# Hybrid encoder layer: the per-head norm of the delta-rule branch summed through VectorE's 32x32 block turn, its later steps ordered behind the solver's instructions, and one tile moved to another ring

## Chip, cores and metric

The kernel runs on one core of one Trainium2 chip. The metric is the device time of one execution in microseconds (us); the median of several runs counts. A core has five engines that run side by side, each through its own instructions in a fixed order: TensorE (PE in the profile, with its weight loads listed apart as PEld), VectorE (DVE), ScalarE (ACT), GpSimd (POOL) and SyncE (SP), which here issues nearly all DMAs.

## The reference

One encoder layer for 512 tokens (two sequences of 256) of 1024 channels, in f32. After an RMS norm and one wide projection come three branches: A, a bidirectional gated delta rule with 8 heads of 128 channels; B, multi-head latent attention with 8 heads and a rotary part; C, cross-attention into 256 memory tokens with 4 heads. Each branch is multiplied by a silu gate, projected, weighted by a sigmoid gate and summed; an output projection, the residual and a final norm follow. What the change is about is the norm at the end of branch A, over the 128 channels of each head and token:

```python
def _rmsnorm(x, gain):
    xf = x.astype(jnp.float32)
    y = xf * lax.rsqrt(jnp.mean(xf * xf, axis=-1, keepdims=True) + EPS)
    return (y * gain.astype(jnp.float32)).astype(x.dtype)
...
    o_gdn = _rmsnorm(o_fwd + o_bwd, gdn_norm_gain).reshape(b, s, W_GDN).astype(x.dtype) * jax.nn.silu(z_gdn)
```

## The kernel before

**Tiling.** Activations lie with channels on the 128 partitions and the 512 tokens along the row. Every projection (`gemm`, L262 to L279) is a set of 128x128 by 128x512 products. Each operand is split into a rounded high part and a low rest, and three products (high x high, low x high, high x low) are summed. For a weight tile ScalarE makes the high part (L241) and VectorE the low part (L244), just ahead of its products. These two steps are remembered as `self.wround` and `self.wsplit`.

**Stages.** `front` does the memory branch, the norms, the decay terms and the latent attention. `middle` does the delta rule with projections woven in. `back` does the last projections and the output. Queues of ready projections (`fills`, `weave`) are put between the dependent steps so that TensorE always has work.

**Order.** In `front` and `back` a scheduler orders each engine's instructions by priority and by a timeline that it estimates. In `middle` TensorE's order is written by a planner, `weave`: each chain of steps is a generator, whose `yield a, b` says that its products cost `a` us of TensorE and that the chain may go on `b` us after them; in between, products from the queue are placed. The other engines are ordered by the scheduler, and the chains have priorities: solver lanes and `heads_out` 2000, `heads_norm` 1500, `heads_in` 300, `preps` 100, queue work below that. `tc.issue_after(x)` makes every instruction traced inside it stand behind `x` on the engine of `x`; it does not concern other engines.

**The chain of one head in `middle`.** `gdn_in` loads decay rows and values and makes the products `kk` (L1015), one group for each half sequence; VectorE multiplies them by decay factors into `ne` (L1025, four instructions a half), which frees the PSUM banks for the next `kk`. `gdn_solve` runs in two lanes (even and odd heads), with VectorE steps at L1117 and `w` at L1136 and ScalarE copies `ub` at L1144. `gdn_out` makes the head's output `o` (L1165), scales it by gain and gate into `og` (L1172), squares it (`sq`, L1174) and adds a small term (L1177). Then come the sums over channels: four products (L1181), one for each 128 tokens, with the squares as 128x128 weights and a column of ones as the moving operand. Their result is 128x4, tokens on partitions. VectorE scales it into `rr` (L1183), GpSimd raises it to the power -1/2 (L1184), VectorE turns `rr` by 32x32 blocks into `rt` (L318), and four DMAs (L320) write the 512 factors to DRAM. `gdn_norm` loads them back as a row on all partitions (`rob`, L324), multiplies (`og`, L1197, behind `wsplit`) and splits the product into `xg` (L252, L256), the operand of the branch's projection `gm_bg` (L1295, L1302, and L276 in `back`).

**Rings.** Scratch tiles of one tag share a ring of buffers: `tb` has 2, `s2` has 5. A new tile waits until all readers of the tile that had its buffer are done. `sq` and `rob` are `tb` tiles. So is `rps` in `decay_b` (L632), which holds the decay rows until DMAs (L638, L639) have written them to DRAM, and so are `rt` and `ru` in `mla_rope`, the rotary part of the queries of four heads. (The name `rt` is used for two tiles: this one, and the turned `rr`.)

**Rotary step.** `mla_rope(g)` makes two projections `ra`, `rb` and then two halves, each two rotations (L524), a sum (L694), a split (L252, L254) and six DMAs (L700 to L706). It is a generator: the second half is traced later, between the key and the query projection of the group's first head.

Of the kernel before, what the change touches and what calls it, by code (L numbers as in the profile page):

```python
# [181 lines left out]
class Layer:  # L182
# [131 lines left out]

    def store_cols(self, r, i):

        nc = self.nc
        nc.vector.transpose(out=self.rt, in_=r)  # L318
        for b in range(4):
            nc.sync.dma_start(self.d_n[i].rearrange("(j b i) -> b j i", j=4, b=4)[b], self.rt[32 * b:32 * b + 4])  # L320

    def load_row(self, dst, i):
# [268 lines left out]
    def decay_b(self):  # L591
# [21 lines left out]
        for s in range(2):  # L613
            for d in range(2):
# [12 lines left out]
                for tb in range(2):  # L627
                    for i in range(2):
                        nc.tensor.matmul(rp[:, s * 256:(s + 1) * 256], ga[:, i, tb],
                                         um[1 + d][:, 128:384] if tb == 0 else um[1 + d][:, 0:256],  # L630
                                         start=d + tb + i == 0, stop=d + tb + i == 3)
        rs = self.tb("rps")  # L632
        nc.scalar.activation(rs, rp, AF.Copy)
# [47 lines left out]
    def mla_rope(self, g):  # L681
# [6 lines left out]
        for j, (p1, p2, op) in enumerate(((pa, pb, ALU.subtract), (pb, pa, ALU.add))):  # L688
            if j:
                yield  # L690
            t, u = self.tb("rt"), self.tb("ru")
            self.rotate(t, unpaired(p1), self.cos)
            self.rotate(u, unpaired(p2), self.sin)
            nc.vector.tensor_tensor(t, t, u, op=op)  # L694
            hi = self.pa.tile([P, 512], F32R, tag="Qn", bufs=4, name=f"rh{g}{j}")
            lo = self.pa.tile([P, 512], F32R, tag="Qn", bufs=4, name=f"rl{g}{j}")
            with self.tc.issue_after(self.wround) if j else nullcontext():
                self.split(t, hi, lo)
            q1, q2, dq = qs1.bitcast(F32), qs2.bitcast(F32), self.d_q[g, j]
            nc.sync.dma_start(dq[0], hi.bitcast(F32))  # L700
            nc.sync.dma_start(dq[1], lo.bitcast(F32))
            for o in (32 * j, 64 + 32 * j):
                nc.sync.dma_start(q1[o:o + 32], dq[0].rearrange("(h r) t -> r h t", h=4))
            for a in range(2):
                o = 64 * a + 32 * j
                nc.sync.dma_start(q2[o:o + 32], dq[1, 64 * a:64 * a + 64].rearrange("(h r) t -> r h t", h=2))  # L706
        self.qs = qs1, qs2
        yield

# [274 lines left out]
    def gdn_in(self, hh):  # L984
# [23 lines left out]
        for s in range(2):  # L1008
# [9 lines left out]
            for d in range(2):  # L1018
                for cp in range(2):
                    cch = cp if d == 0 else 1 - cp  # L1020
                    w = 4 * h + 2 * s + cch
                    r = slice(256, 384) if cp else slice(0, 256)
                    kin = pc[cch][:, :, 128 * (1 - d):128 * (2 - d)] if cp else pc[cch]
                    n = 128 if cp else 256
                    nc.vector.scalar_tensor_tensor(  # L1025
                        ne[:, :, d, s, r], es[d][:, s, r].unsqueeze(1).to_broadcast([P, 2, n]),
                        cc[:, d, w:w + 1], kin, ALU.mult, ALU.mult)
        nc.gpsimd.tensor_tensor(v3, v3, nk[:, 4 * h:4 * h + 4].unsqueeze(2).to_broadcast([P, 4, P]), op=ALU.mult)  # L1028
# [3 lines left out]
    def gdn_solve(self, hh):  # L1032
# [72 lines left out]
        for cp in range(2):  # L1105
# [29 lines left out]
            wv = w2(f"w2{hh}{cp}")  # L1135
            nc.vector.tensor_tensor(wv, v4[:, :, 1 - cp], x3, op=ALU.subtract)  # L1136
            yield 0.45, 6.5
# [4 lines left out]
            for d in range(2):  # L1142
                t = slice(64 * (1 - d), 64 * (1 - d) + 64)
                nc.scalar.activation(ub[t, d, :, cp], u3[t], AF.Copy)  # L1144
            yield 0.45, 6.5
        self.ub[hh] = ub

    def gdn_out(self, hh):
# [28 lines left out]
        nc.vector.tensor_tensor(s3, s3, kq[:, :, 1], op=ALU.add)  # L1177
        yield 0.0, 13 if hh == 7 else 11
        ssp = self.ps_ms(par, f"so{hh}")
        for tb in range(4):  # L1180
            nc.tensor.matmul(ssp[:, tb:tb + 1], sq[:, tb * P:(tb + 1) * P], c("one"), start=True, stop=True)  # L1181
        rr = self.rr[:, 0:4]
        nc.vector.tensor_scalar(rr, ssp[:, 0:4], 1.0 / 128, 128 * EPS * EPS, ALU.mult, ALU.add)  # L1183
        nc.gpsimd.tensor_tensor(rr, rr, c("hf")[:, 0:4], op=ALU.pow)  # L1184
        self.store_cols(self.rr, hh)
        self.og[hh] = og, self.now + 10.0
        yield 0.9, 0.0

    def gdn_norm(self, hh):
# [5 lines left out]
        yield 0.0, 6.0 if hh == 7 else 12.0  # L1195
        with self.tc.issue_after(self.wsplit):
            nc.vector.tensor_tensor(og, og, rb, op=ALU.mult)  # L1197
        hl = self.pk.tile([P, 2, 512], F32R, tag="kq", bufs=8, name=f"xg{hh}")
        self.split(og, hl[:, 0], hl[:, 1], 0.5)
        self.xg[hh] = hl[:, 0], hl[:, 1]  # L1200
# [268 lines left out]
    def front(self):  # L1469
# [24 lines left out]
        self.mem_attn(3, *q)  # L1494
        rope = self.mla_rope(0)
        next(rope)
        for g in range(2):
            fills(1)
            self.mla_v(g)

            def between():
                next(rope)
                fills(1)

            nxt = self.mla_qk(4 * g, between)
            for h in range(4):
# [12 lines left out]
                if h == 3 and g == 0:  # L1519
                    rope = self.mla_rope(1)  # L1520
                    next(rope)
                    fills(1)
# [5 lines left out]
    def middle(self):  # L1528
# [6 lines left out]
        for j in range(2):  # L1535
# [4 lines left out]
            self.ym.append((y, m))  # L1540
        self.started, self.b0 = set(), None
        self.og, self.b0 = {}, self.blocks(0)
# [166 lines left out]
```

## Time and profile before

| what | value |
|---|---|
| median of 3 runs | 808.98 us (808.81, 808.98, 810.21) |
| profiled execution: its time | 810.45 us |
| profiled execution: span of its instructions | 808.6 us |
| granted TensorE clock over the span | 0.996 |
| busy share of the span: PE, PEld, DVE, ACT, POOL | 98%, 87%, 70%, 55%, 18% |
| DMA: moved, mean rate | 118.20 MB, 146 GB/s |

How to read the rows below. In a timeline, each row is: start in us, duration in us, engine, line of the kernel, operation, output<-inputs, shape, count (xN: N in a row, first start to last end); a bracket holds the idle time of the engine just before the row and what ended it. In a table of groups the figures after the bar are total busy us and mean ns of one instruction, then idle time before them. Waits are: engine and line, what it waited for, us in total, times, longest. Windows are: stretch, its length, then busy us and count for PE, PEld, DVE, ACT and POOL, then the granted TensorE clock, DMA share and GB/s. A product of f32 operands shows as two records, one of the rounded kind as one.

### The profile page before, as it was taken

The page shows a single profiled execution, that of the slowest core. Times are in us where ns is not written, and L with a number is a line of the kernel's source. Part 1 is how long each engine was busy: PE and PEld are TensorE (multiplying, and loading weights), DVE is VectorE, ACT ScalarE, POOL GpSimd, SP SyncE. Part 2 cuts the span into 40 slices and gives each one's busy share as a digit, 9 for nine tenths or more (in the row PEclk, how much of TensorE's full clock was granted, in tenths as well). Part 3 has the DMA queues.
Part 4 walks back from the last instruction along what each step waited for, and adds up shares of the span by engine and source line. Part 5 has one row for each costly group of instructions (what it writes and reads, how often), then busy time and mean ns, then how long its engine had stood idle before and what let it go on. Part 6 is the DMA issues. An engine that isn't in the chain of part 4 may idle for free.

```text
span 808.6 us, 13182 instructions
## 1 busy us (share of the span) xinstructions
PE 794.3 (98%) x4822; PEld 699.7 (87%) x4822; DVE 565.6 (70%) x957; ACT 448.8 (55%) x895; POOL 147.1 (18%) x135
## 2 busy tenths in 40 slices
PE   9999999999999999999999999999999999999996
PEld 7888888889898889988888878788888888888885
DVE  7786458688699999577699998666644654455543
ACT  7755455456565566648676748476755552222332
POOL 0200111000010002074032136214110002223221
PEclk9999999999999999999999999999999999999999
DMA  9422222552417625345344353736444557454532
GB/s 333 162 81 95 92 91 76 185 150 74 120 60 228 162 98 168 123 153 168 118 131 139 109 174 127 216 124 180 149 129 130 182 196 251 131 185 173 172 104 105
DMA packets 68913, 118.20 MB, mean 146 GB/s; under 512 B 23664, under 2 KB 31216, under 8 KB 68848
## 3 DMA queue, kind: packets, MB, share of 16 engines
q1 hardware_dynamic: 67552, 115.00, 45.2%
q10 hardware_dynamic: 1296, 2.36, 0.8%
q8 instruction: 38, 0.62, 0.3%
q14 instruction: 27, 0.22, 0.1%
HBM read 98.24 MB, written 19.09 MB: 145 GB/s over the span
## 4 chain that ended last, share of the span: by engine, by line
PE 86%; DVE 8%; DMA 2%; ACT 2%; issue 1%; SPq 0%; POOL 0%; POOLq 0%; DVEq 0%; ACTq 0%
PE gm_g L276 14%; PE gm_qkv L276 12%; PE gm_z L276 5%; PE gm_za L276 5%; PE gm_bm L276 5%; PE y L1328 4%; PE vm L429 3%; PE gm_be L276 3%; PE gm_qm L276 3%; PE gm_km L276 3%; PE gm_bg L276 3%; PE o L1165 2%; PE gm_bg L1295 2%; PE s_a L337 2%; PE kk L1015 2%; PE gm_qn L276 2%
## 5 line engine op out<-in xcount | busy, mean ns | idle before, releaser
L782 DVE SCALAR_TENSOR_TENSOR kq<-cz,prm,kq 128x510 f32<-128x510 f32 (+1 forms) x64 | 52.7, 823 | 3.7 <-ACT kq L775 2.9
L276 PE MATMUL gm_qkv<-hh,wh_qkv 128*128 128x512 f32 x192 | 49.2, 389 | 1.3 <-ACT wh_qkv L241 1.3
L276 PE MATMUL gm_g<-hh,wl_g 128*128 128x512 f32 x192 | 48.9, 384 | 0.0
L276 PE MATMUL gm_g<-hl,wh_g 128*128 128x512 f32 x192 | 48.1, 384 | 0.0
L276 PE MATMUL gm_g<-hh,wh_g 128*128 128x512 f32 x192 | 48.1, 385 | 0.0
L276 PE MATMUL gm_qkv<-hl,wh_qkv 128*128 128x512 f32 x192 | 47.7, 383 | 0.0
L276 PE MATMUL gm_qkv<-hh,wl_qkv 128*128 128x512 f32 x192 | 47.4, 383 | 0.0
L244 DVE TENSOR_TENSOR wl_g<-wr_g,wh_g 128x1024 fp32r<-128x1024 f32 x24 | 29.8, 1243 | 19.4 <-PE gm_g L276 10.2
L276 PEld LDWEIGHTS gm_qkv<-hh,wh_qkv 128*128 128x128 f32 x192 | 35.9, 192 | 6.5 <-ACT wh_qkv L241 1.7
L1025 DVE SCALAR_TENSOR_TENSOR ne<-e,cc,kk 128x512 f32<-128x512 f32 (+1 forms) x64 | 35.5, 607 | 8.3 <-PE kk L1015 5.6
L276 PEld LDWEIGHTS gm_qkv<-hh,wl_qkv 128*128 128x128 f32 x192 | 35.9, 189 | 4.9
L276 PEld LDWEIGHTS gm_qkv<-hl,wh_qkv 128*128 128x128 f32 x192 | 35.7, 189 | 4.7
L276 PEld LDWEIGHTS gm_g<-hl,wh_g 128*128 128x128 f32 x192 | 35.5, 189 | 4.8
L276 PEld LDWEIGHTS gm_g<-hh,wl_g 128*128 128x128 f32 x192 | 35.3, 189 | 4.5
L276 PEld LDWEIGHTS gm_g<-hh,wh_g 128*128 128x128 f32 x192 | 35.1, 189 | 4.6
L244 DVE TENSOR_TENSOR wl_qkv<-wr_qkv,wh_qkv 128x1024 fp32r<-128x1024 f32 x24 | 30.9, 1286 | 10.6 <-ACT wh_qkv L241 5.3
L1328 PE MATMUL y<-wh_wo,mh 128*128 128x512 f32 (+1 forms) x144 | 37.7, 356 | 0.0
L1270 POOL TENSOR_TENSOR mg<-mg,lg 128x512 f32<-128x512 f32 x16 | 27.0, 1695 | 50.5 <-DVE lg L1269 29.7
L241 ACT ACTIVATE wh_qkv<-wr_qkv 128x1024 fp32r<-128x1024 f32 x24 | 25.3, 1055 | 19.2 <-DMA wr_qkv<-in_w_dram 6.8
L241 ACT ACTIVATE wh_g<-wr_g 128x1024 fp32r<-128x1024 f32 x24 | 25.3, 1054 | 17.4 <-PE gm_g L276 12.4
L1028 POOL TENSOR_TENSOR vs<-vs,ns 128x512 f32<-128x512 f32 x8 | 8.5, 1065 | 128.0 <-DVE tt L911 84.4
L997 POOL TENSOR_TENSOR kl<-kq,kh 128x512 fp32r<-128x512 f32 x16 | 22.5, 1410 | 50.0 <-ACT kh L995 47.7
(453 smaller groups left out, 2187.5 us busy)
## 6 DMA issues: line engine op xcount, KB each, us to landing
wr_g<-in_w_dram SPq DMA_DIRECT2D x24, 512.0 KB
wr_qkv<-in_w_dram SPq DMA_DIRECT2D x24, 512.0 KB
e<-d_r SPq DMA_DIRECT2D x64, 96.0 KB
wr_z<-in_w_dram SPq DMA_DIRECT2D x12, 512.0 KB
d_g<-gt_g SPq DMA_DIRECT2D x16, 256.0 KB
wr_za<-in_w_dram SPq DMA_DIRECT2D x8, 512.0 KB
lg<-d_g SPq DMA_DIRECT2D x16, 256.0 KB
wr_bm<-in_w_dram SPq DMA_DIRECT2D x8, 512.0 KB
```

The costliest lines, as they stand in the source:

```text
L241: self.wround = nc.scalar.activation(hi[:, :n], raw[:, :n], AF.Copy).ins
L244: self.wsplit = nc.vector.tensor_tensor(lo[:, :n], raw[:, :n], hi[:, :n].bitcast(F32), op=ALU.subtract).ins
L276: nc.tensor.matmul(pairs(ps[:m]), a[:, k * m:(k + 1) * m], turns(xs[k][j]), start=n == 0, stop=n == 3 * nk - 1)
L337: nc.tensor.matmul(pairs(sp[:, qb * 256:(qb + 1) * 256]), a, turns(b), start=j == 0, stop=j == n - 1)
L429: nc.tensor.matmul(pairs(vps[tb]), ms[k][a][:, t], turns(b[:, :512]), start=k == 0 and i == 0, stop=k == 7 and i == 2)
L782: nc.vector.scalar_tensor_tensor(ys, zs, self.cw[:, f, m:m + 1], ys, ALU.mult, ALU.add)
L997: nc.gpsimd.tensor_tensor(lo, src, hi.bitcast(F32), op=ALU.subtract)
L1015: nc.tensor.matmul(pairs(ps), a[:, k], turns(b), start=i == 0, stop=i == 2)
L1025: nc.vector.scalar_tensor_tensor(ne[:, :, d, s, r], es[d][:, s, r].unsqueeze(1).to_broadcast([P, 2, n]), cc[:, d, w:w + 1], kin, ALU.mult, ...
L1165: nc.tensor.matmul(out, ub[:, d, s, cp], rhs, start=n == 0, stop=n == 3)
L1270: nc.gpsimd.tensor_tensor(self.merged[d], self.merged[d], gt, op=ALU.add)
L1328: nc.tensor.matmul(pairs(ps), xs[2 * j + q][a][:, t], turns(b[:, q * 512:(q + 1) * 512])[:, c0 // 2:c1 // 2], start=j == 0 and n == 0, sto ...
```

## The change

In `gdn_out` VectorE now turns the 128x512 squares by 32x32 blocks (`st`) and adds up each group of 32 along the row, which leaves 128x16 partial sums. One product with a 128x32 block-identity as weights adds the four partition groups, 32x16. The power step works on 32x16; the store becomes one turn of 32x32 and one DMA. The store is a step of its own, 4 us (head 7: 2 us) after the power step. The planner's waits change from 11 to 12 us before the product, and from 10 to 8 us before the row may be loaded; the product's stated cost falls from 0.9 to 0.25.

A list `kept` holds the last eight traced instructions of three kinds: `ne` (L1025), `w` (L1136) and the `ub` copies (L1144). `behind()` orders what is traced in it after `wsplit` and after all of these. It covers the turn and the sum, the turn of the factors, and in `gdn_norm` both the multiplication and the split.

`rps` moves from ring `tb` to ring `s2`. `mla_rope` is no longer a generator: both halves are traced at once, and the second one's split is no longer ordered behind `wround`.

```diff
-        rs = self.tb("rps")
+        rs = self.s2("rps")
...
         for j, (p1, p2, op) in enumerate(((pa, pb, ALU.subtract), (pb, pa, ALU.add))):
-            if j:
-                yield
...
-            with self.tc.issue_after(self.wround) if j else nullcontext():
-                self.split(t, hi, lo)
+            self.split(t, hi, lo)
...
-        yield 0.0, 13 if hh == 7 else 11
+        st = self.tb(f"st{hh}")
+        red = self.rr[:, 16:32]
+        with self.behind():
+            nc.vector.transpose(out=st, in_=sq)
+            nc.vector.tensor_reduce(red, st.rearrange("p (j i) -> p j i", i=32), axis=AX.X, op=ALU.add)
+        yield 0.0, 13 if hh == 7 else 12
         ssp = self.ps_ms(par, f"so{hh}")
-        for tb in range(4):
-            nc.tensor.matmul(ssp[:, tb:tb + 1], sq[:, tb * P:(tb + 1) * P], c("one"), start=True, stop=True)
-        rr = self.rr[:, 0:4]
-        nc.vector.tensor_scalar(rr, ssp[:, 0:4], 1.0 / 128, 128 * EPS * EPS, ALU.mult, ALU.add)
-        nc.gpsimd.tensor_tensor(rr, rr, c("hf")[:, 0:4], op=ALU.pow)
-        self.store_cols(self.rr, hh)
-        self.og[hh] = og, self.now + 10.0
-        yield 0.9, 0.0
+        nc.tensor.matmul(ssp[0:32, 0:16], c("i32"), red, start=True, stop=True)
+        rr = self.rr[0:32, 0:16]
+        nc.vector.tensor_scalar(rr, ssp[0:32, 0:16], 1.0 / 128, 128 * EPS * EPS, ALU.mult, ALU.add)
+        nc.gpsimd.tensor_tensor(rr, rr, c("hf")[0:32, 0:1].to_broadcast([32, 16]), op=ALU.pow)
+        yield 0.25, 2.0 if hh == 7 else 4.0
+        with self.behind():
+            nc.vector.transpose(out=self.rt[0:32], in_=self.rr[0:32])
+        nc.sync.dma_start(self.d_n[hh].rearrange("(j i) -> j i", i=32), self.rt[0:16])
+        self.og[hh] = og, self.now + 8.0
+
+    def keep(self, i):
+        self.kept = (self.kept + [i])[-8:]
+
+    @contextmanager
+    def behind(self):
+        with ExitStack() as st:
+            for i in [self.wsplit] + self.kept:
+                st.enter_context(self.tc.issue_after(i))
+            yield
...
-        with self.tc.issue_after(self.wsplit):
+        with self.behind():
             nc.vector.tensor_tensor(og, og, rb, op=ALU.mult)
-        hl = self.pk.tile([P, 2, 512], F32R, tag="kq", bufs=8, name=f"xg{hh}")
-        self.split(og, hl[:, 0], hl[:, 1], 0.5)
+            hl = self.pk.tile([P, 2, 512], F32R, tag="kq", bufs=8, name=f"xg{hh}")
+            self.split(og, hl[:, 0], hl[:, 1], 0.5)
```

More of the change, by code (lines that the diff above doesn't have):

```diff
@@ L1 @@
-from contextlib import ExitStack, nullcontext
+from contextlib import ExitStack, contextmanager, nullcontext
 import numpy as np
@@ L313, in bcast @@
                                   self.c("id"), start=True, stop=True)
[L315 to L320, printed above, removed]
     def load_row(self, dst, i):
@@ L707, in mla_rope @@
         self.qs = qs1, qs2
-        yield
     def mla_v(self, g):
@@ L1024, in gdn_in @@
                     n = 128 if cp else 256
-                    nc.vector.scalar_tensor_tensor(
+                    nev = nc.vector.scalar_tensor_tensor(
                         ne[:, :, d, s, r], es[d][:, s, r].unsqueeze(1).to_broadcast([P, 2, n]),
-                        cc[:, d, w:w + 1], kin, ALU.mult, ALU.mult)
+                        cc[:, d, w:w + 1], kin, ALU.mult, ALU.mult).ins
+                    self.keep(nev)
         nc.gpsimd.tensor_tensor(v3, v3, nk[:, 4 * h:4 * h + 4].unsqueeze(2).to_broadcast([P, 4, P]), op=ALU.mult)
@@ L1135, in gdn_solve @@
             wv = w2(f"w2{hh}{cp}")
-            nc.vector.tensor_tensor(wv, v4[:, :, 1 - cp], x3, op=ALU.subtract)
+            self.keep(nc.vector.tensor_tensor(wv, v4[:, :, 1 - cp], x3, op=ALU.subtract).ins)
             yield 0.45, 6.5
@@ L1143, in gdn_solve @@
                 t = slice(64 * (1 - d), 64 * (1 - d) + 64)
-                nc.scalar.activation(ub[t, d, :, cp], u3[t], AF.Copy)
+                self.keep(nc.scalar.activation(ub[t, d, :, cp], u3[t], AF.Copy).ins)
             yield 0.45, 6.5
@@ L1494, in front @@
         self.mem_attn(3, *q)
-        rope = self.mla_rope(0)
-        next(rope)
+        self.mla_rope(0)
         for g in range(2):
@@ L1499, in front @@
             self.mla_v(g)
[L1501 to L1505, printed above, removed]
+            nxt = self.mla_qk(4 * g, lambda: fills(1))
             for h in range(4):
@@ L1519, in front @@
                 if h == 3 and g == 0:
-                    rope = self.mla_rope(1)
-                    next(rope)
+                    self.mla_rope(1)
                     fills(1)
@@ L1540, in middle @@
             self.ym.append((y, m))
-        self.started, self.b0 = set(), None
+        self.started, self.b0, self.kept = set(), None, []
         self.og, self.b0 = {}, self.blocks(0)
```

## The prediction

> **What bounds the kernel now.** I read the page's busy times first, then TensorE's waits, then windows over the stretches with idle time, then timelines around those.
>
> ```profile
> PE 794.3 (98%) x4822; PEld 699.7 (87%) x4822; DVE 565.6 (70%) x957; ACT 448.8 (55%) x895; POOL 147.1 (18%) x135
> ```
>
> TensorE is busy for 794.3 us of a span of 808.6, so 14.3 us are idle. Only two things can move the end by much: less time on TensorE, or less of that idle time.
>
> ```profile
> PE kk L1015 <- DVE ne L1025: 3.3, 3, 1.7
> PE zp L397 <- DVE zero L394: 1.5, 1, 1.5
> PE gm_qkv L276 <- ACT wh_qkv L241: 1.3, 1, 1.3
> ```
>
> ```profile
> 470.00:480.00 10.00, 8.48 (x44) 6.96 (x43) 8.73 (x17) 4.53 (x9) 4.67 (x3) 1.00 0.72 194
> 510.00:520.00 10.00, 8.25 (x32) 6.54 (x31) 9.13 (x14) 5.14 (x11) 4.55 (x4) 0.83 0.78 204
> 515.60:519.00 3.40, 3.27 (x10) 2.76 (x11) 3.40 (x6) 0.63 (x1) 1.27 (x2) 0.53 0.56 150
> 800.00:808.60 8.60, 1.60 (x15) 1.41 (x13) 1.60 (x5) 1.55 (x5) 1.28 (x2) 0.85 0.32 123
> ```
>
> Of the 14.3 us, 7.0 lie in the tail (8.60 less 1.60) and 1.5 at the start (`zp`); the change reaches neither. It can reach the waits for `ne` (3.3, in the first two windows) and for `wh_qkv` (1.3). The third window shows a loss that does not count as idle: right after the longest wait the granted clock is 0.53 for 3.4 us, 1.6 us of work lost.
>
> **The product.** One head's four calls, between the rows of a steady stream, and the nearest row with 32 columns of weights:
>
> ```profile
> 713.60 1.03 PE L276 MATMUL gm_bm<-xa,wh_bm 128*128 128x512 f32 x4
> 714.47 0.95 PE L1181 MATMUL so<-cst,sq 128*128 128x1 f32 x8
> 715.28 0.46 PE L276 MATMUL gm_bm<-xa0h,wl_bm 128*128 128x512 f32 x1
> 715.58 0.59 PE L276 MATMUL gm_bm<-xa,wl_bm 128*128 128x512 f32 x2
> ```
>
> ```profile
> 401.61 1.30 PE L861 MATMUL kd<-kq 128*32 128x32 f32 x128
> ```
>
> Four ordinary products start over 0.87 us (713.60 to 714.47), 0.22 each. From `so` to 715.58 pass 1.11 us; less 0.22 for the product between, the four `so` calls cost 0.89, or 0.22 a call. One call stays. Its upper bound is that 0.22. Its lower bound is `kd`: 1.30/128 = 0.01 a record, 0.02 a call, but `kd` fills four column strips side by side. I take four times that, 0.08, since the new weights have `kd`'s shape. Saved per head: 0.81 (0.67 to 0.87), over 8 heads **6.5 us** (5.4 to 7.0), all on the engine that sets the end. The Trainium skill (TensorE: Matmul & The Clock Gate, LDWEIGHTS) says that a weight load takes time by its columns, columns/1.2 ns; by that my estimate is 0.05 for the two records and 6.7 us saved.
>
> **What VectorE and GpSimd get.**
>
> ```profile
> L807 DVE STREAM_TRANSPOSE vt<-vf 128x512 f32<-128x512 f32 x8 | 5.6, 703 | 0.0
> L340 DVE TENSOR_REDUCE mx_a<-s_a 128x2 f32<-128x512 f32 x16 | 10.9, 683 | 4.6 <-PE s_a L337 3.9 <-PE gm_za L276 0.6
> L881 POOL TENSOR_TENSOR nk<-k,cst 128x16 f32<-128x16 f32 x2 | 5.8, 2898 | 87.4 <-DVE k L873 87.4
> L1184 POOL TENSOR_TENSOR rr<-rr,cst 128x4 f32<-128x4 f32 x8 | 9.5, 1186 | 110.0 <-DVE rr L1183 77.9 <-DMA wr_bm<-in_w_dram 32.1
> ```
>
> A turn (0.70) and a sum (0.68) are 1.39 us more VectorE work per head, 11 us in all on an engine that is busy for 70%. They stand between the squares and the product. The power step has 16 columns instead of 4: by the two POOL rows it takes between 1.2 and 2.9 us, and I take 2.9, the row with 16 columns. VectorE's turn of the factors waits for it, with `ne`, `w` and weight splits queued behind; that turn is now a step 4 us later, which covers 2.9. Were that cover gone, VectorE would stand still for up to 1.7 us more a head. Three of four store DMAs go, which only shortens SP's queue. On ScalarE the rounding of `xg` now stands behind `ub` copies that were traced before it; nobody waits for `xg` before `gm_bg` (rival 3). From the outputs to the multiplication the planner waits 36.25 us instead of 33.9 (head 7: 29.25 for 29.9).
>
> **The two `ne` waits.**
>
> ```profile
> 477.44 0.45 PE L1015 MATMUL kk<-kh 128*128 128x512 f32 x1 [1.36 <-DVE ne L1025]
> ...
> 515.73 0.69 PE L1015 MATMUL kk<-kh 128*128 128x512 f32 x1 [1.74 <-DVE ne L1025]
> ```
>
> ```profile
> 473.64 0.69 DVE L1197 TENSOR_TENSOR og<-og,rob 128x512 f32<-128x512 f32 x1 [0.95 <-DMA rob<-d_n]
> ...
> 475.56 0.68 DVE L256 SCALAR_TENSOR_TENSOR xg<-og,xg 128x512 fp32r<-128x512 f32 x1
> 476.17 2.18 DVE L1025 SCALAR_TENSOR_TENSOR ne<-e,cc,kk 128x512 f32<-128x512 f32 x4
> ...
> 510.62 0.69 DVE L1197 TENSOR_TENSOR og<-og,rob 128x512 f32<-128x512 f32 x1 [2.93 <-DMA rob<-d_n]
> 511.23 0.68 DVE L1207 SCALAR_TENSOR_TENSOR zt_z<-zt_z,gm_z 128x512 f32<-128x512 f32 x1
> 511.82 1.13 DVE L1025 SCALAR_TENSOR_TENSOR ne<-e,cc,kk 128x512 f32<-128x512 f32 x2
> 512.88 1.66 DVE L256 SCALAR_TENSOR_TENSOR xg<-og,xg 128x512 fp32r<-128x512 f32 x1
> ```
>
> Both have one cause. VectorE's fixed order holds an earlier head's norm (`og`, `xg`), for which nobody waits, ahead of the `ne` for which TensorE waits; it even stands still for the norm's row (0.95 and 2.93 us). In the planner's order each half's `ne` is traced 5 us after its second `kk`, and the multiplication only 0.9+10+12 us after `so`, which is later here. So these `ne` are among the eight kept, and `behind()` puts `og` and `xg` after them.
>
> At 477.44 this takes 0.95+0.69+0.68 = 2.32 us from in front of `ne`. If all of the new 1.39 lies in front instead, and TensorE comes 0.81 sooner, only 0.12 is won; if gaps on VectorE take the 1.39 in, the whole 1.36 goes. I take the middle, about **0.8**. At 515.73, 2.93+1.66 go, which exceeds the wait of 1.74 by more than 1.39+0.81: I take the whole **1.74** (0 at worst).
>
> **The front.**
>
> ```profile
> 150.05 0.69 DVE L524 TENSOR_TENSOR ru<-rb,sin 128x512 f32<-128x512 f32 x1 [5.43 <-DMA d_r<-rps]
> ```
>
> ```profile
> 162.53 1.78 PE L276 MATMUL gm_qkv<-hh,wh_qkv 128*128 128x512 f32 x7 [1.28 <-ACT wh_qkv L241]
> ```
>
> `ru` had to wait for the `tb` buffer of `rps`, whose DMAs had not landed, and VectorE stood for 5.43 us. The chain of waits runs from there through VectorE and ScalarE to the wait at 162.53. In ring `s2`, with 5 buffers, the 5.43 go. The second rotary half (four VectorE steps, a split on two engines, six DMAs on SP) comes sooner and may now stand ahead of weight splits and roundings; it is old work, and the freed 5.43 us hide it. I book the whole **1.3**; if that cover fails, nothing is won.
>
> **Sum.** 6.5 + 0.8 + 1.74 + 1.3 = 10.3 us. The profiled execution took 810.45, 1.85 over its span; less 10.3 and the 1.6 of half clock it would take 798.55. The median is 808.98. There I leave the clock loss out, because the profiled execution is 1.47 above it, as if the others had not paid it: 808.98 - 10.3 = **798.7 us**. The window puts the half clock right behind a wait of 1.74 us. The Trainium skill (TensorE: Matmul & The Clock Gate, What's actually happening) says that the clock halves after an idle window of some 3.4 us; by that so short a wait would not be its cause, the 1.6 would stay in the profiled execution (800.15), and the median's sum would not change.
>
> **Rivals.** *1. The `ne` waits stay*, because VectorE is the bound around them and 1.39 us more per head takes what was won.
>
> ```profile
> 460.00:470.00 10.00, 10.00 (x52) 8.88 (x51) 9.73 (x26) 7.87 (x18) 1.07 (x1) 1.00 0.33 119
> ```
>
> For it: VectorE is busy for 9.73 of these 10 us. Against it: TensorE waits for nothing here, so what fills VectorE can wait. If it holds, what heads 0 and 1 save lies ahead of the two waits and is lost in them too: 10.3 - 2.54 - 1.62 = 6.1, time 802.8; with the front unpaid and one more 1.39 it is 805.5. Chance 0.24. That `behind()` binds nothing, the eight entries having been overwritten by two lanes, would look the same and is counted here.
>
> *2. Slower: TensorE waits at the small product.* It needs the turn and the sum, which are bound behind a weight split and eight others.
>
> ```profile
> 452.90 0.68 DVE L1177 TENSOR_TENSOR sq<-sq,kq 128x512 f32<-128x512 f32 x1
> ...
> 458.56 0.95 PE L1181 MATMUL so<-cst,sq 128*128 128x1 f32 x8
> ...
> 463.72 0.17 DVE L1183 TENSOR_SCALAR rr<-so 128x4 f32<-128x4 f32 x1
> ```
>
> The squares end at 453.58 and the product starts at 458.56, now one planner us later: 6.0 us, less 1.39, leave 4.6. For it: VectorE came to `rr` 4.2 us after `so` had ended (459.51), so it does lag. Also, three `tb` tiles a head now share two buffers, so the turn of one head waits for the multiplication of the head before (473.64, 21 us after its squares, with heads some 37 us apart: 473.64 to 510.62). It decides when each head's sum comes 10.3/8 = 1.3 us past the margin; a lag of 4.6 + 1.7 costs 8 x 1.7 = 13.6, time 812.3. Against it: all that the sum is bound behind was traced earlier, and TensorE needs most of it sooner. Chance 0.06.
>
> *3. The tail takes some back:* `xg` of head 7 comes too late for `gm_bg`.
>
> ```profile
> 729.49 0.69 DVE L256 SCALAR_TENSOR_TENSOR xg<-og,xg 128x512 fp32r<-128x512 f32 x1 [0.69 <-ACT xg L252]
> ```
>
> ```profile
> 736.51 0.81 PE L1302 MATMUL gm_bg<-xg,w_bg 128*128 128x512 f32 x3
> ```
>
> It is ready 6.3 us early. The power step adds 1.7 at most, the binds perhaps two weight splits and their DMAs. If it comes 9 us later, 2.7 are lost: 801.4. Chance 0.08.
>
> *4. No change:* TensorE's saved time comes back as other waits of the same size, 808.98. For it: 11 us of VectorE work are added. Against it: outside the two windows TensorE waits for VectorE almost nowhere. Chance 0.04.
>
> **Numbers.** The forecast has 0.58. The range goes from 795.8 (7.0, 3.3, 1.3 and the clock's 1.6: 13.2) to rival 1's 805.5; rivals 2 and 4 lie outside. About 0.2% of the time, 1.6 us, is what a measurement of this kernel can tell from no change. Faster: 0.58 + 0.24 + 0.08, less 0.02 for ends worse than rival 1 gives, 0.88; same 0.04 + 0.01, slower 0.06 + 0.01.
>
> **What would show it.** Right: TensorE is busy for 6 to 8 us less (the half clock included); `so` has 16 records; its waits name neither `wh_qkv` near 162 nor `ne` for 1.7; the 5.43 at `ru` is gone; `og` and `xg` of heads 0 and 1 stand behind `ne`. Wrong: TensorE waits at `so` or at `gm_bg`, weight splits wait behind turns, or `ne` comes as late as before.

## The result and the profile after

| | before | after |
|---|---|---|
| median, first comparison | 808.89 us (808.04 to 810.21) | 803.38 us (802.27 to 803.68) |
| median, measured again beside the last experiments | 808.93 us (807.84 to 810.63) | 803.15 us (802.27 to 804.72) |
| ratio | | 0.9932, 95% interval 0.992 to 0.9945 (again: 0.9932, 0.9919 to 0.9945) |
| profiled execution, span | 810.45, 808.6 us | 803.32, 801.5 us |

The change makes the kernel 5.5 to 5.8 us faster. Forecast were 10.3 us less (798.7). First the page's busy times of the changed kernel, then TensorE's waits (what waited, what it waited for, us in all, times, longest):

```profile
PE 789.8 (99%) x4774; PEld 693.1 (86%) x4774; DVE 575.4 (72%) x973; ACT 448.9 (56%) x895; POOL 165.2 (21%) x135
```

```profile
PE u L1112 <- ACT y L1089: 2.0, 1, 2.0
PE zp L390 <- DVE zero L387: 1.5, 1, 1.5
PE vm L422 <- ACT wh_vm L413: 0.6, 1, 0.6
```

The waits for `ne` (3.3 us) and for `wh_qkv` and `wl_kn` (1.3 and 0.3) are gone. TensorE has 48 records fewer, as it should (8 heads, 3 calls, 2 records each), and is busy for 4.5 us less (794.3 to 789.8); the prediction had named 6 to 8 us as a sign of being right. New is a wait of 2.0 us of `u` for the `y` copies. The next windows (start and end, length, busy time and count of PE, PEld, DVE, ACT and POOL, granted clock, DMA share, GB/s) show what comes behind it. The first is the changed kernel's profiled execution, the second another execution of the same kernel:

```profile
570.00:580.00 10.00, 8.43 (x36) 7.36 (x37) 6.83 (x14) 6.93 (x17) 3.43 (x2) 0.83 0.34 116
```

```profile
570.00:580.00 10.00, 8.05 (x44) 7.04 (x43) 8.51 (x17) 8.09 (x20) 4.49 (x2) 1.00 0.30 106
```

With a granted clock of 0.83 over 10 us, 1.7 us of work are lost on top of the wait; with 1.00 nothing is. So one and the same wait does not always bring the clock down.

The product, in the stretch of steady products (the same place as in the prediction):

```profile
711.53 0.81 PE L1301 MATMUL gm_bg<-xg,w_bg 128*128 128x512 f32 x3
712.27 0.23 PE L1175 MATMUL so<-rr,cst 128*32 128x16 f32 x2
712.43 1.35 PE L1301 MATMUL gm_bg<-xg,w_bg 128*128 128x512 f32 x5
```

From 711.53 to 712.43 pass 0.90 us; three ordinary products take 0.65 of that (0.22 each). One `so` call costs 0.25 us, not 0.08. Saved per head: 0.89 - 0.25 = 0.64, or 5.1 us if the other seven heads save as much as this one.

VectorE's and GpSimd's new steps, by groups (count, then busy us and mean ns of one):

```profile
L1171 DVE STREAM_TRANSPOSE st<-sq 128x512 f32<-128x512 f32 x8 | 5.6, 706 | 0.1
L1172 DVE TENSOR_REDUCE rr<-st 128x16 f32<-128x512 f32 x8 | 5.4, 680 | 0.1
L1178 POOL TENSOR_TENSOR rr<-rr,cst 32x16 f32<-32x16 f32 x8 | 25.2, 3148 | 71.5 <-DVE rr L1177 71.5
```

These are nearly the sizes that were booked (0.70, 0.68, and 2.9 for the power step, whose mean is 3.1). And VectorE's order around head 0, whose norm stood ahead of `ne` before (473.64 and 475.56, `ne` at 476.17):

```profile
473.28 2.19 DVE L1014 SCALAR_TENSOR_TENSOR ne<-e,cc,kk 128x512 f32<-128x512 f32 x4
...
480.51 2.14 DVE L1014 SCALAR_TENSOR_TENSOR ne<-e,cc,kk 128x512 f32<-128x512 f32 x4
482.58 0.68 DVE L1203 TENSOR_TENSOR og<-og,rob 128x512 f32<-128x512 f32 x1
483.95 0.69 DVE L256 SCALAR_TENSOR_TENSOR xg<-og,xg 128x512 fp32r<-128x512 f32 x1 [0.70 <-ACT xg L252]
```

The norm is now behind the `ne` of both halves, and nobody on TensorE waited for it.

### The profile page after: what moved, and what is told of

The parts are those of the page before. It is cut to its first block, busy times and chain, and to the rows that moved or that the text cites. A ratio compares the mean times of both kernels' runs of the same rounds, so it can differ in the third digit from the quotient of the medians.

```text
span 801.5 us, 13067 instructions
## 1 busy us (share of the span) xinstructions
PE 789.8 (99%) x4774; PEld 693.1 (86%) x4774; DVE 575.4 (72%) x973; ACT 448.9 (56%) x895; POOL 165.2 (21%) x135
## 4 chain that ended last, share of the span: by engine, by line
PE 93%; DMA 2%; ACT 2%; issue 1%; SPq 1%; DVE 0%; POOL 0%; POOLq 0%; ACTq 0%; DVEq 0%
PE gm_qkv L276 16%; PE gm_g L276 14%; PE gm_z L276 7%; PE gm_za L276 5%; PE gm_bm L276 5%; PE y L1334 5%; PE gm_be L276 3%; PE gm_qm L276 3%; PE gm_km L276 3%; PE gm_bg L276 3%; PE kk L1004 2%; PE gm_bg L1301 2%; PE o L1155 2%; PE s_a L330 2%; PE vm L422 2%; PE gm_qn L276 2%
## 5 line engine op out<-in xcount | busy, mean ns | idle before, releaser
L1178 POOL TENSOR_TENSOR rr<-rr,cst 32x16 f32<-32x16 f32 x8 | 25.2, 3148 | 71.5 <-DVE rr L1177 71.5
L244 DVE TENSOR_TENSOR wl_qkv<-wr_qkv,wh_qkv 128x1024 fp32r<-128x1024 f32 x24 | 31.7, 1322 | 10.3 <-ACT wh_qkv L241 3.8
```

Of the source, the lines that this page charges most:

```text
L244: self.wsplit = nc.vector.tensor_tensor(lo[:, :n], raw[:, :n], hi[:, :n].bitcast(F32), op=ALU.subtract).ins
L1178: nc.gpsimd.tensor_tensor(rr, rr, c("hf")[0:32, 0:1].to_broadcast([32, 16]), op=ALU.pow)
```

## The experiments

Times are medians, each with the kernel before measured on the same chip in the same set: 808.82 us in the first set of four, 808.92 in the second, 808.93 in the third.

| kernel | us | ratio to before (95%) |
|---|---|---|
| `front_part` | 808.20 | 0.9995 (0.9985 to 1.0006) |
| `norm_order` | 808.65 | 1.0003 (0.9993 to 1.0012) |
| `product4` | 804.60 | 0.9951 (0.9936 to 0.9965) |
| `xe_late` | 802.42 | 0.9926 (0.9911 to 0.9940) |
| `ring_only` | 807.52 | 0.9985 (0.9976 to 0.9994) |
| `rope_back` | 801.77 | 0.9914 (0.9900 to 0.9927) |
| `rope_back_xe_late` | 799.99 | 0.9893 (0.9880 to 0.9907) |
| `unbound` | 801.28 | 0.9907 (0.9891 to 0.9922) |
| `after_again` | 803.15 | 0.9932 (0.9919 to 0.9945) |
| `unbound_early` | 808.45 | 0.9991 (0.9981 to 1.0000) |
| `unbound_best` | 800.14 | 0.9887 (0.9875 to 0.9900) |
| `sum2` | 810.65 | 1.0016 (0.9996 to 1.0036) |

### The product: `product4`

The changed kernel, with the small product made four times over:

```diff
-        nc.tensor.matmul(ssp[0:32, 0:16], c("i32"), red, start=True, stop=True)
+        for _ in range(4):
+            nc.tensor.matmul(ssp[0:32, 0:16], c("i32"), red, start=True, stop=True)
```

> The changed kernel with the small product made four times in a row (same operands, same result), which adds 24 calls to TensorE. If a call costs 0.25 us, as the gap in the stream of products after the change suggests, 6.0 us more: about 809.4. If it costs 0.08, as was predicted from the kd row, 1.9 us more: about 805.3. If TensorE's time were not the bound, no difference: 803.4.

Measured: 804.60, 1.2 to 1.5 us over the changed kernel (803.38 and 803.15). The two intervals overlap, so the reading rests on the timeline at the same place:

```profile
713.40 0.81 PE L1302 MATMUL gm_bg<-xg,w_bg 128*128 128x512 f32 x3
714.14 0.43 PE L1176 MATMUL so<-rr,cst 128*32 128x16 f32 x8
714.49 1.35 PE L1302 MATMUL gm_bg<-xg,w_bg 128*128 128x512 f32 x5
```

From 713.40 to 714.49 pass 1.09 us; less 0.65, four calls cost 0.44. One costs 0.25, so three more cost 0.19, or 0.06 each; 8 x 0.19 is 1.5 us, which the measured time allows. A further call is as cheap as the prediction took it (0.08). What it left out is the rest of the 0.25, about 0.19 us that the group costs once, between the wide product ahead of it and the one behind it. What makes up these 0.19 was not tested.

By the Trainium skill (TensorE: Matmul & The Clock Gate, LDWEIGHTS), a weight load's time follows its columns; that estimate was 0.05 for the call's two records. The measured 0.06 for a further call agrees; the 0.19 is not in that rule. The trace's own records of these weight loads last 0.11 us each (0.19 before, with 128 columns), so it is the spacing of the calls that agrees and not the length of a record.

### The two front edits: `front_part`, `ring_only`, `rope_back`

`front_part` is the kernel before with both edits that reach the front: `rps` in the other ring, and the two halves of the rotary traced at once.

```diff
-        rs = self.tb("rps")
+        rs = self.s2("rps")
...
-            if j:
-                yield
...
-        rope = self.mla_rope(0)
-        next(rope)
+        self.mla_rope(0)
...
-            nxt = self.mla_qk(4 * g, between)
+            nxt = self.mla_qk(4 * g, lambda: fills(1))
```

> The kernel before with the front's part of the change alone: rps in ring s2, both rotary halves at once. Theory A (the parts add up): the wait of 5.43 us at ru and TensorE's waits for wh_qkv (1.28) and wl_kn (0.28) go, the rest stays, 1.3 to 1.6 us less: about 807.4. Theory B (only the removed TensorE work counts, and a wait that goes comes back later): 808.9, with a new wait of about 1.5 us further on.

Measured: 808.20 against 808.82, no difference that can be told, though 1.3 us of waits are gone. The wait came back 110 us later: 1.2 us of `gm_qn` for `kn` at 271 us, which the kernel before does not have. Other kernels with both edits show it too, with 0.3 to 2.0 us, but the first profile of the changed kernel and `unbound` (below) do not. What lies ahead of it, on SP's queue in the changed kernel:

```profile
257.53 0.34 SPq L691 DMA_DIRECT2D d_q<-rl  x1
262.15 0.79 SPq L693 DMA_DIRECT2D qs<-d_q  x2
...
264.51 0.41 SPq L229 DMA_DIRECT2D wr_qn<-in_w_dram  x1
```

The four reads `qs` of the rotary's second half wait 4.3 us at the head of the queue, until the stores of the same half have landed, and the load of the weights `wr_qn` is queued behind them. The second execution of the changed kernel shows the end of that chain, on ScalarE and on TensorE:

```profile
268.94 0.52 ACT L241 ACTIVATE wh_qn<-wr_qn 128x384 fp32r<-128x384 f32 x1 [3.83 <-DMA wr_qn<-in_w_dram]
```

```profile
271.43 0.89 PE L276 MATMUL gm_qn<-qlh,wh_qn 128*128 128x512 f32 x3 [0.98 <-DVE kn L254]
```

ScalarE stands for 3.83 us for the load, and the split of `kn`, for which TensorE waits, is queued behind. The next two kernels tell whether this is the cause. `ring_only` is the kernel before with only the first line pair of the diff above:

> The kernel before with one edit: the decay rows' tile `rps` in the other ring. Theory A: the 1.3 and 0.3 us waits for `wh_qkv` and `wl_kn` go, and since the rotary's second half stays where it was, the load of `wr_qn` is still issued ahead of its four reads, so no wait of `gm_qn` for `kn` comes at 272 us: 1.0 to 1.6 us less than before, about 807.4 of 808.8. Theory B: the time gained is lost in the same stretch whatever the rotary does (the stretch is bound by its loads): `gm_qn` waits 1 to 2 us for `kn`, and the time is 808.2 to 808.8, as it was with both front edits.

`rope_back` is the changed kernel with the second half back in its place, and only the ring edit left at the front:

```diff
+            if j:
+                yield
...
-        self.mla_rope(0)
+        rope = self.mla_rope(0)
+        next(rope)
...
-            nxt = self.mla_qk(4 * g, lambda: fills(1))
+            def between():
+                next(rope)
+                fills(1)
+
+            nxt = self.mla_qk(4 * g, between)
```

> The changed kernel with the rotary's second half traced again between the two halves of the first scores' products; the decay rows' tile stays in its new ring. Theory A: in the changed kernel the load of `wr_qn` stands on SP's queue behind four reads of the second half, which wait 4.6 to 5.9 us for their own stores; with the half back in its place the load is issued ahead of them, ScalarE's rounding of `wr_qn` waits under 1 us instead of 3.0 to 4.4, and the wait of `gm_qn` for `kn` (0 to 2.0 us, three of four profiles) goes: about 1.2 us less than the changed kernel, 802.2. Theory B: the order on the queue decides nothing: the wait is still there, and the time is the changed kernel's, 803.4.

Measured: `ring_only` 807.52, 1.4 us less than before, and TensorE's longest waits in it are

```profile
PE kk L1015 <- DVE ne L1025: 3.1, 3, 1.8
...
PE s_m L337 <- ACT p_m L351: 0.5, 1, 0.5
```

with neither `wh_qkv` nor `gm_qn` among them. `rope_back` took 801.77, 1.4 to 1.6 us less than the changed kernel. SP's queue and ScalarE in it:

```profile
260.83 0.37 SPq L694 DMA_DIRECT2D d_q<-rl  x1
261.40 0.33 SPq L229 DMA_DIRECT2D wr_qn<-in_w_dram  x1
262.97 0.79 SPq L696 DMA_DIRECT2D qs<-d_q  x2
```

```profile
265.84 0.52 ACT L241 ACTIVATE wh_qn<-wr_qn 128x384 fp32r<-128x384 f32 x1
```

The load is issued ahead of the reads, 3.1 us sooner, and ScalarE waits for nothing. The times alone would not name the queue as the cause: the intervals of `ring_only` and `front_part` overlap, and `rope_back` (four runs from 800.90 to 802.30, the changed kernel's ten from 802.27 to 804.72) also brings back the second split's order behind `wround` and shifts some of TensorE's own products in the front. What names it is that two waits go together over all traces. ScalarE's wait for `wr_qn` and TensorE's wait for `kn` are

| kernel | ScalarE for `wr_qn`, us | TensorE for `kn`, us |
|---|---|---|
| `ring_only`, `rope_back`, `rope_back_xe_late` | none | none |
| `unbound` | 2.47 | none |
| changed kernel, first profile | 2.98 | none |
| `unbound_early` | 3.17 | 0.3 |
| changed kernel, second profile | 3.83 | 1.0 |
| `front_part` | 4.05 | 1.2 |
| `xe_late`, `sum2` | 4.43 | 1.6 |
| `product4` | 4.83 | 2.0 |

TensorE waits for what is over about 2.9 us of ScalarE's wait. So Theory A holds in both: the ring edit is worth its 1.3 to 1.4 us, and the rotary's move takes 0.7 (`front_part` over `ring_only`, not resolved) to 1.6 us (`rope_back`) back. A part of `rope_back`'s gain may be the clock, which stayed at 1.00 around 570 us in its profile.

### The norm's binding and its due time: `norm_order`, `unbound`, `unbound_early`

`norm_order` is the kernel before with the binding in `gdn_norm` alone (`keep` and `behind` as in the change):

```diff
-        with self.tc.issue_after(self.wsplit):
+        with self.behind():
             nc.vector.tensor_tensor(og, og, rb, op=ALU.mult)
-        hl = self.pk.tile([P, 2, 512], F32R, tag="kq", bufs=8, name=f"xg{hh}")
-        self.split(og, hl[:, 0], hl[:, 1], 0.5)
+            hl = self.pk.tile([P, 2, 512], F32R, tag="kq", bufs=8, name=f"xg{hh}")
+            self.split(og, hl[:, 0], hl[:, 1], 0.5)
```

> The kernel before with behind() in gdn_norm alone: the multiplication and the split of the norm stand behind the last ne, w and ub; sums and store as before. Theory A: the waits for ne (1.36, 0.16, 1.74) go, 3.3 us less, and up to 1.6 more in executions that had the half clock: 804 to 805.6. Theory B (VectorE is the bound there, whatever the order): the waits for ne stay at 2.5 us or more, or come back elsewhere: 808 to 809.

Measured: 808.65, no change. The 3.3 us of `kk` waits are gone, and these have come:

```profile
PE u L1123 <- ACT y L1100: 0.9, 2, 0.6
PE us L1142 <- DVE w L1137: 0.8, 1, 0.8
PE xs L1133 <- ACT u L1125: 0.8, 1, 0.8
...
PE p L1067 <- DVE ne L1025: 0.5, 2, 0.3
```

They add up to 3.0. So the binding alone does take the norm out from in front of `ne`, with the early due time of the kernel before, but the waits move from this step of a lane to others. Does it do better inside the change? `unbound` is the changed kernel with the binding taken out everywhere. TensorE's order is the same, instruction for instruction:

```diff
-        with self.behind():
+        with nullcontext():
             nc.vector.transpose(out=st, in_=sq)
...
-        with self.behind():
+        with nullcontext():
             nc.vector.transpose(out=self.rt[0:32], in_=self.rr[0:32])
...
-        with self.behind():
+        with self.tc.issue_after(self.wsplit):
             nc.vector.tensor_tensor(og, og, rb, op=ALU.mult)
```

> The changed kernel without its binding of the norm's steps: turn, sum and the turn of the factors are bound to nothing, the multiplication only to the last weight split as before. TensorE's order is the same, instruction for instruction; only VectorE's and ScalarE's orders differ (norms ahead of `ne` in most heads). Theory A: the binding is what removed the `ne` waits; without it 2 to 3.3 us of waits for `ne` return, and the 1.96 us wait of `u` may go: 803.4 to 806. Theory B: the binding only moves waits about, as it did when it was put into the kernel before by itself (0.2 us better there): the time stays within 0.7 us of 803.4.

Measured: 801.28, about 2 us less than with the binding, which neither theory had expected. TensorE's longest waits in it, apart from `zp`, and VectorE's order around head 0:

```profile
PE u L1112 <- ACT y L1089: 1.2, 1, 1.2
PE vm L422 <- ACT mh L252: 0.8, 1, 0.8
```

```profile
472.75 2.19 DVE L1014 SCALAR_TENSOR_TENSOR ne<-e,cc,kk 128x512 f32<-128x512 f32 x4
...
477.10 0.68 DVE L1203 TENSOR_TENSOR og<-og,rob 128x512 f32<-128x512 f32 x1
```

The norm is behind the `ne` in question without any binding (head 1 likewise: `ne` at 507.42, `og` at 511.06). The remaining candidate is the planner: from the outputs to the multiplication it now waits 36.25 us where it waited 33.9. `unbound_early` takes those 2.35 us back and changes nothing else:

```diff
-        self.og[hh] = og, self.now + 8.0
+        self.og[hh] = og, self.now + (8.0 if hh == 7 else 5.65)
```

> The changed kernel without its binding, and with the planner's due time of the multiplication 2.35 us earlier for heads 0 to 6 (5.65 us after the turn of the factors instead of 8.0), which restores the 33.9 us of the kernel before from outputs to multiplication. TensorE's order is the same, instruction for instruction; on VectorE `og` and `xg` of the first two heads stand ahead of `ne` again. Theory A: it is the later due time that took the norm out from in front of `ne`, not the binding; so with the early one the waits of `kk` for `ne` return, 2.5 to 3.3 us: 803.8 to 804.6, against 801.3 without the binding alone. Theory B: what removed these waits is the shorter path to the row `rob` (one store instead of four, on a shorter queue), so that `og` no longer stands still ahead of `ne`; then the time stays at 801.3 within 0.7 us, and waits of `kk` for `ne` stay under 0.8 us.

Measured: 808.45, 7.2 us more than `unbound`. Its first wait, VectorE at the two places, and the window behind the first:

```profile
PE kk L1004 <- DVE ne L1014: 5.1, 4, 2.5
```

```profile
475.01 0.69 DVE L1203 TENSOR_TENSOR og<-og,rob 128x512 f32<-128x512 f32 x1 [3.74 <-DMA rob<-d_n]
...
476.30 1.13 DVE L1014 SCALAR_TENSOR_TENSOR ne<-e,cc,kk 128x512 f32<-128x512 f32 x2
...
513.93 0.69 DVE L1203 TENSOR_TENSOR og<-og,rob 128x512 f32<-128x512 f32 x1 [3.31 <-DMA rob<-d_n]
...
516.00 2.17 DVE L1014 SCALAR_TENSOR_TENSOR ne<-e,cc,kk 128x512 f32<-128x512 f32 x4
```

```profile
476.00:486.00 10.00, 6.74 (x26) 5.59 (x27) 9.97 (x18) 5.15 (x12) 6.67 (x4) 0.83 0.43 129
```

VectorE stands 3.74 and 3.31 us for the norm's row with `ne` queued behind. TensorE loses 5.1 us in waits for `ne`, and a clock of 0.83 over 10 us costs another 1.7. Other waits are shorter than in `unbound` (`u` 0.4 for 1.2, `vm` 0.4 for 0.8, `p` none for 0.4), and `gm_qn` has 0.3. That makes 5.5 of the 5.6 us by which the two profiled spans differ (805.1 and 799.5); why the medians differ by 7.2 is not shown. The expectation had the mechanism but less than half of the size. So without the binding the removal of the `ne` waits is shown to hang on the later due time. Either of the two is enough to keep the norm behind `ne`: the due time by `unbound`, the binding by `norm_order`. The change has both.

Does the binding cost the 2 us? All four runs of `unbound` (800.47 to 801.55) lie below all ten of the changed kernel (802.27 to 804.72). Since TensorE's order is the same, the traces can be laid beside each other. The small product `so` starts, in us, at

| execution | head 0 | head 3 | head 4 |
|---|---|---|---|
| changed kernel, first profile | 458.43 | 565.08 | 612.13 |
| changed kernel, second profile | 459.16 | 565.69 | 611.07 |
| `unbound` | 458.14 | 565.50 | 610.14 |

At head 0 the second execution is 1.0 us behind `unbound`, by the `gm_qn` wait at 271 us, which comes ahead of every bound step. From head 0 to head 3 the binding gains 0.7 to 0.8 us. From there to head 4, with the wait of `u` between, it loses 0.7 again, and in the first profile another 1.7 by the clock. So the traces do not show that the bound order itself costs 2 us. They show a longer wait of `u` (1.96 for 1.21), behind which the clock falls in one of two executions, and a wait in the front that is not the binding's. What the 2 us of the medians consist of stays open.

### The new wait at 571 us: `xe_late`

ScalarE in the changed kernel ahead of the wait, and the two products on TensorE between which it lies:

```profile
567.87 2.17 ACT L252 ACTIVATE xe<-xe 128x512 fp32r<-128x512 f32 x4
...
570.43 1.09 ACT L1089 ACTIVATE y<-yp 32x128 f32<-32x128 f32 x4
```

```profile
560.79 0.45 PE L1081 MATMUL yp<-y,p1s 32*32 32x32 f32 x32
...
571.57 0.71 PE L1112 MATMUL u<-vs,y 128*128 128x128 f32 x4 [1.96 <-ACT y L1089]
```

`yp` is there at 561.2, and its copies start at 570.43 behind four `xe` roundings (2.17 us). The same order stood in the kernel before, where TensorE came to `yp` 6.2 us later and waited for no copy:

```profile
567.02 0.45 PE L1091 MATMUL yp<-y,p1s 32*32 32x32 f32 x32
```

`xe_late` puts the roundings behind the copies:

```diff
-        with self.tc.issue_after(self.wround):
+        with self.tc.issue_after(self.wround), self.tc.issue_after(self.ycopy):
             for hi, lo in xs:
...
-                nc.scalar.activation(
+                self.ycopy = nc.scalar.activation(
-                                     AF.Copy)
+                                     AF.Copy).ins
```

> The changed kernel with the four splits of xe put behind the lane's y copies on ScalarE. TensorE's order stays the same. Theory A (the new wait of 1.96 us of u for y comes from these splits being ahead of y on ScalarE): the wait goes, and with it the half clock behind it: 2.0 to 3.6 less, 799.8 to 801.4. Theory B (the wait is VectorE's vs step, or the splits are needed just as soon by gm_be): the wait stays or turns up at gm_be, 803.4.

Measured: 802.42. Against the changed kernel's 803.15 to 803.38 that is 0.7 to 1.0 us, within what the intervals leave open; but in its profile the wait is gone and the clock is 1.00 throughout 570 to 580. That profile has the `gm_qn` wait, with 1.6 us. Together with `rope_back` the edit's effect is clearer:

> The changed kernel with the rotary's second half back in its place and the four `xe` roundings behind the lane's `y` copies on ScalarE. Theory A: the waits at 272 us and at 571 us have separate causes, so the two edits add: 1.0 (measured alone for the second) and 1.2 less than the changed kernel's 803.4, so 801.2, and TensorE waits nowhere over 0.6 us between the start and the tail. Theory B: the time gained in one place is lost in the next, since the lanes' chain sets the pace: 802.4, the time with the second edit alone, and other waits of together 1 to 2 us appear.

Measured: 799.99, 1.8 us under `rope_back` and 3.2 under the changed kernel. TensorE's longest waits are

```profile
PE zp L390 <- DVE zero L387: 1.5, 1, 1.5
PE x L1106 <- ACT ub L1138: 0.7, 1, 0.7
```

so both waits are gone, the two causes are separate, and their removals add: 1.4 to 1.6 and 0.7 to 1.0 us alone, 3.2 together, where 2.2 was expected. `unbound_best` takes the binding out as well:

> The changed kernel without its binding, with the rotary's second half back in its place and the `xe` roundings behind the lane's `y` copies. Theory A: the three edits remove waits in three places and add as far as they do not overlap; the binding's cost lies partly in the 571 us wait that the `xe` edit removes too, so 0 to 1.5 us under the 800.0 of the two edits with the binding: 798.5 to 800.0. Theory B: without the binding some norm stands ahead of a lane's step again once the `xe` roundings are moved, and it is no better than 800.0.

Measured: 800.14, the same within the intervals. Once the waits at 272 and at 571 us are gone, the binding costs nothing. That agrees with the three traces above, in which the kernels with and without it differ mainly by these two places. `rope_back_xe_late` and `unbound_best` both beat the two kernels compared here, by 3 us and by almost 9.

### VectorE's room: `sum2`, and `after_again`

`sum2` makes the turn and the sum twice:

```diff
             nc.vector.transpose(out=st, in_=sq)
             nc.vector.tensor_reduce(red, st.rearrange("p (j i) -> p j i", i=32), axis=AX.X, op=ALU.add)
+            nc.vector.transpose(out=st, in_=sq)
+            nc.vector.tensor_reduce(red, st.rearrange("p (j i) -> p j i", i=32), axis=AX.X, op=ALU.add)
```

> The changed kernel with the block turn and the sum made twice for each head: 1.39 us more on VectorE a head, 11 us in all, between the squares and the product; nothing else changed. Theory A: VectorE has room for them, as for the first turn and sum: no more than 0.7 us over the changed kernel. Theory B: the first turn and sum already used up that room and are part of why only 5.5 of the 10.3 us came; then each head's second pair delays `ne`, `w` or the product, and the time is 3 us or more above the changed kernel, with new waits of TensorE for VectorE.

`after_again` is the changed kernel itself beside it:

> The changed kernel itself, to stand beside the others on one chip. Both theories: 803.4, within 0.7 us. If it comes out at 801.5 or less, then the 2.1 us by which the kernel without the binding was ahead belongs to the chip and not to the binding.

Measured: `after_again` 803.15, within 0.3 us of the first comparison, and the kernel before lies within 0.2 us in the three sets; so chips do not make differences of 2 us here. `sum2` 810.65, 7.5 us more, with runs from 806.49 to 815.58. First the end of head 0's sum on VectorE and its product on TensorE in the changed kernel, then both in `sum2`, with the product of head 1:

```profile
456.64 0.68 DVE L1172 TENSOR_REDUCE rr<-st 128x16 f32<-128x512 f32 x1
```

```profile
458.43 0.23 PE L1175 MATMUL so<-rr,cst 128*32 128x16 f32 x2
```

```profile
461.45 0.68 DVE L1174 TENSOR_REDUCE rr<-st 128x16 f32<-128x512 f32 x1
```

```profile
462.28 0.21 PE L1177 MATMUL so<-rr,cst 128*32 128x16 f32 x2 [2.42 <-DVE rr L1174]
501.05 0.21 PE L1177 MATMUL so<-rr,cst 128*32 128x16 f32 x2 [3.60 <-DVE rr L1174]
```

In the changed kernel the sum ends at 457.32, 1.1 us before the product, the smallest margin of the eight heads (the others have 2.1 to 7.6). The second pair is 1.39 us of work but ends much later than 1.39 us after the first, because VectorE's queue sets other steps between. TensorE waits 6.0 us for the sum in two heads, and behind the longer wait the clock is 0.83 from 500 to 510 us, 1.7 us more. Theory B holds in what it says of doubled work: there is no room for a second pair. The single pair makes no wait of TensorE at `so`.

## Why the forecast came out right in direction and too large

**Bound.** Right. TensorE is busy for 99% of the span, and all that was won is work taken from it or waits removed from it.

**Product.** Right mechanism, wrong size: 5.1 us, from one head's row, instead of 6.5. The step that failed is "I take four times that, 0.08, since the new weights have `kd`'s shape". `kd`'s 128 records stand in one row, so a figure per record holds next to nothing of what a group costs once; one call alone pays all of it, 0.19 us. The bound of 0.22 from the old calls was nearer, but it too was below the measured 0.25, so that the saving fell short of the 5.4 to 7.0 given.

**VectorE and GpSimd.** Sizes right (0.71, 0.68, 2.9 to 3.1). That the turn and the sum are covered was right for the changed kernel, but "6.0 us, less 1.39, leave 4.6" was wrong: it set the steps back to back behind the squares. The sum ended 1.1 us before its product. Rival 2 was much nearer than its 0.06 said; `sum2` shows it. The cover for the power step, "a step 4 us later, which covers 2.9", also failed in part. VectorE stands still for it in five heads, 7.6 us in all (4.9 in six heads before), most in head 4:

```profile
615.57 0.20 DVE L1181 STREAM_TRANSPOSE rt<-rr 32x32 f32<-32x32 f32 x1 [3.01 <-POOL rr L1178]
```

No wait of TensorE is put down to it: in the changed kernel TensorE waits for VectorE only at `zp` (1.5) and at `oa` (0.3).

**The `ne` waits.** All 3.3 us went, more than the 2.54 booked. The reason given, "`behind()` puts `og` and `xg` after them", names a way that works (`norm_order`), but not one that was needed: without the binding the waits stay away (`unbound`), and with 2.35 us less in the planner's due time as well they come back as 5.1 us (`unbound_early`). The prediction had written down the 36.25 and the 33.9 and drew nothing from them.

**The front.** The 5.43 us at `ru` and 1.6 us of TensorE's waits went, but "it is old work, and the freed 5.43 us hide it" failed. The prediction counted the second half's six DMAs on SP, yet did not ask what is queued behind them there: the load of `wr_qn`, behind reads that wait over 4 us for their own stores. `ring_only` (-1.4), `front_part` (no change), `rope_back` (1.4 to 1.6 under the changed kernel) and the table of the two waits show it.

**What came back.** The largest miss is a term that is not in the sum at all. TensorE, 6.2 us earlier by then, reaches `u` before a `y` copy that ScalarE had always made late, and waits 1.96 us. In the profiled execution it loses another 1.7 to the clock.

**The sum as measured.** It closes on the two profiled executions, whose spans differ by 7.1 us (808.6 and 801.5). Gone are `ne` 3.3, the front's waits 1.6 and 0.6 of the tail (idle 7.0 before, 6.4 after); new are `u` 2.0, and `vm` and `x` 0.8. That is 2.7 us less idle time. TensorE's busy time fell by 4.5, near the 5.1 of the product; the half clock, paid in both (1.6 and 1.7), cancels. Together they are 7.2 us. The medians differ by only 5.5 to 5.8, because the profiled execution of the kernel before took 1.5 us more than its median, and that of the changed kernel its median. What the quicker executions of the kernel before did otherwise no trace shows. In the second profile of the changed kernel the clock is kept, and `gm_qn` takes 1.0. So of some 10.6 us won (5.1, 3.3, 1.6 and 0.6), 2.8 to 3.8 were lost again as waits, and in some executions 1.7 more by the clock, most of it in two places away from the head norm.

**Rivals.** Rival 1 had a time range that fits (802.8 to 805.5), but not its mechanism: the `ne` waits did not stay. That the time lies inside the stated range is therefore luck: the range reached so far up for this rival's sake, and no term of the sum stood for the waits that came back. Rival 4's kind of loss did happen in part, but the new waits are for ScalarE and for a load, not for VectorE's added work. Rival 3 did not happen. `xg` of head 7 and its first product in the same group of lines:

```profile
727.05 0.69 DVE L256 SCALAR_TENSOR_TENSOR xg<-og,xg 128x512 fp32r<-128x512 f32 x1 [0.70 <-ACT xg L252]
```

```profile
730.02 0.81 PE L1308 MATMUL gm_bg<-xg,w_bg 128*128 128x512 f32 x3
```

It is ready 2.3 us early, where it had been 6.3; 4 of the 6.3 are gone.

## What to carry to other kernels

On a kernel whose bound engine is busy for 98%, a removed wait counts only as far as the next operand is early: after adding up a saving, move the bound engine forward by it and look for the first step, on any engine or queue, whose operand would then be late. When DMAs are moved earlier, ask for each queue what stands behind a read that waits for its own store. Before steps are bound to an order by hand, look whether a due time already gives that order, and try them apart.

## What the runs showed that I had not expected

- A short f32 product between wide ones costs about 0.19 us once and 0.06 us for each call (128x16 by 32 columns of weights, `product4`).
- Waits of 1.74 us (before), 1.96 (after) and 1.76 (`ring_only`) were followed by a lowered granted clock (0.83 over 10 us after the last two, 0.53 over 3.4 us after the first), and waits of 1.78 (`product4`), 1.80 (`rope_back`), 2.0 (`after_again`) and even 2.42 (`sum2`) by 1.00. Such a wait can cost twice its length or just its length; what decides was not found. The Trainium skill (TensorE: Matmul & The Clock Gate, What's actually happening) puts the halving at an idle window of some 3.4 us. These runs show it behind single waits of half that, so here the measurement decides. The same section says that the window runs freely and does not start anew with the kernel. That would fit one and the same wait with two outcomes, but no run here shows where the windows lay.
- In the kernel without the binding, a planner's due time earlier by 2.35 us costs 7.2 us by the medians (`unbound_early`), more than the whole change brought.
